# Three elementwise products of a layer moved from GpSimd to VectorE, and the recurrences' output, square and last-chain steps moved back in the order of work

## The chip, the cores and the metric

The kernel runs on one core of a Trainium2 chip. TensorE (PE) multiplies matrices into banks of PSUM; VectorE (DVE), ScalarE (ACT) and GpSimd (POOL) do elementwise work; SyncE (SP) issues most DMAs. Each engine works through its own instructions in a fixed order. The metric is the device time of one execution in microseconds; lower is better.

## The reference

One layer of a hybrid decoder, on 1024 positions of width 1024, in float32:

```
u     = rms_norm(x);  proj = u @ w_in             # 1024 -> 3584: q, k, v and hq, hf, hi, hg
attn  = rms_norm(dilated_attention(q, k, v))      # 8 heads of 64, three dilated windows merged
# HGRN2, 4 heads of 128, chunkwise:
forget = lb + (1 - lb) * sigmoid(hf);  b = cumsum(log(forget)) in a chunk
q_dec  = silu(hq) * exp(b);  k_inv = (1 - forget) * exp(-b)
rec    = tril(q_dec k_inv^T) @ hi + q_dec @ state;  state = decay * state + k_end^T @ hi
rec    = rms_norm(rec) * silu(hg)
h   = x + concat(attn, rec) @ w_out
h   = h + conv_glu(rms_norm(h))                   # 1024 -> 2 x 2816 -> 1024, causal conv of width 3
out = rms_norm(h)
```

## The kernel before, in words

Every float32 operand of a large product is split into an upper part (a rounded copy) and a lower part (what the copy leaves), and each product is three matmuls (upper by upper, upper by lower, lower by upper). ACT mostly makes the copies and DVE or POOL the subtractions. Activations lie transposed: 128 features on the partitions, 512 positions (a half, hf = 0 or 1) along a row.

The stages are: input projection and attention (0 to 303 us of the trace), the recurrences with their projections (303 to 484), the output projection (from 484, the last recurrences within it), the gated mixer up and down, and the final norm. PE's instructions run in the order in which the program writes them. The order on the other engines is planned ahead from a model of costs, among the instructions that the model holds ready, with those written earlier first; an instruction wrapped in `keep_in_program_order` stays behind the one written before it on its engine.

In the recurrence stage the filler work is 24 half projections (list HG: forget "hf", query "hq", gate "hg", 4 heads by 2 halves). Each is a `dense` of 24 matmuls into one of two banks ("mm"), which a DVE multiplication empties (L718, L732, L745). Behind it stand a sigmoid of three ACT activations (`sigmoid`, L708 to L710) and a product that makes the gate. Between the fillers the program puts the steps of eight recurrences, called chains 0 to 7 here, for (head, half) = (0,0), (0,1), (1,0), (1,1), (2,0), (3,0), (2,1), (3,1). A place is counted in half projections; `play` runs the filler up to a step's place and then writes the step. From place 24 on the filler is the output projection (`out_pair`). The five steps of a chain (`recur`) are:

1. scans over the log gates, differences, three exponentials on ACT (ex, C, A; L808, L811, L812), the query's product with the decay (E times C, L813) and the key's (B times A, L814);
2. four transposes (psK) and eight small matmuls of scores (psA); ACT copies kT, DVE masks into AT;
3. four matmuls for psU; DVE scales them and runs the state along the chunks (U, st; L839 to L847);
4. four or eight matmuls for the outputs psO, from AT and from st; ACT squares them (hsq, L860);
5. a matmul by ones sums the squares (hss, L863); ACT and DVE make the reciprocal root (`rstd_part`, L314 to L318), DVE scales psO by it (rhy, L865), POOL multiplies by the gate (L867).

The tiles rs_y (first st, then rhy) and rs_m (first U, then the square and rht) have one buffer each, so a chain's states wait for the tail of the chain before. The norm of the attention output (`attn_norm`) runs beside the first chains, at places 0.25 to 4.25 and 7 to 11; it makes the output projection's upper and lower operands attn_hi and attn_lo (L769 to L771). A chain of number n has at = 4.5 + 3n; its first step stood at the place just behind its query projection, step 2 at `at`, step 3 at `at + 1`, step 4 at `at + 2` (`at + 2.3` for chains 6 and 7) and step 5 at `at + 2.8`. For chain 0, steps 2 to 4 stood 0.5 later.

Of the kernel before, what the change touches and what calls it, by code (L numbers as in the profile page):

```python
# [12 lines left out]
AF = mybir.ActivationFunctionType  # L13
# [29 lines left out]
def f32(ap):  # L43
    return ap.bitcast(F32)
# [157 lines left out]
def hybrid_kernel(ctx: ExitStack, tc: tile.TileContext, xT, w_qk, w_tok, w_hg, w_out, w_up,  # L202
                  w_down, vecs, amask, hmask, out):
    nc = tc.nc
    PE, DVE, ACT, POOL = nc.tensor, nc.vector, nc.scalar, nc.gpsimd
# [93 lines left out]
    def col(j):  # L299
        return vec[:, j : j + 1]  # L300
# [24 lines left out]
    def vtile(shape, dt, name):  # L325
        return rv.tile(shape, dt, tag="v", name=name, bufs=2)
# [10 lines left out]
    def bank(tag, name):  # L337
        return ps1.tile([P, H2], F32, tag=tag, name=name, bufs=2)
# [4 lines left out]
    at = at_cm.__enter__()  # L343
# [347 lines left out]
    attn_lo = mix.tile([P, 4, SEQ], F32R, name="attn_lo")  # L691
    rec_hi0 = mix.tile([P, 4, H2], F32R, name="rec_hi0")
    def gtile(name, dt=F32):
        return mix.tile([P, H2], dt, tag="g", name=name, bufs=4)

    attn_hi = vtile([P, 4, SEQ], F32R, "attn_hi")
# [3 lines left out]
    with pool("hg", "right") as hg:  # L700
# [3 lines left out]
        def ht(tag, nm, bufs=1):  # L704
            return hg.tile([P, H2], F32, tag=tag, name=nm, bufs=bufs)

        def sigmoid(dst, src):
            ACT.activation(dst, src, AF.Exp, scale=-1.0)  # L708
            ACT.activation(dst, dst, AF.Ln, bias=1.0)
            ACT.activation(dst, dst, AF.Exp, scale=-1.0)  # L710
# [17 lines left out]
        def q_half(h, hf, last):  # L728
            def evac(ps):
                nm = f"{h}_{hf}"  # L730
                E, F = ht("E", "E" + nm, 2), ht("F", "F" + nm)
                DVE.tensor_mul(E, ps, R1[:, halves[hf]])  # L732
                DVE.tensor_scalar_max(F, E, -40.0)
                sigmoid(F, F)
                POOL.tensor_mul(E, E, F)
                gate[h, hf].append(E)
            return dense(("hq", h), hf, evac, last)

# [14 lines left out]
        def attn_norm(hf):  # L753
            t = halves[hf]
            acc, s2 = gtile(f"asq{hf}"), gtile(f"asq{hf}_s")
            ACT.activation(acc, raw[0, hf], AF.Square)
            for c in range(1, 4):
                ACT.activation(s2, raw[c, hf], AF.Square)
                DVE.tensor_add(acc, acc, s2)
            yield  # L760
            ss = bank("t", f"ass{hf}")
            PE.matmul(ss, ones, acc, start=True, stop=True)
            R = rstd_part(acc, s2, ss, 1.0 / 512)
            yield
            for c in range(4):
                if c == 2:
                    yield
                a = raw[c, hf]
                DVE.scalar_tensor_tensor(a, a, col(V_AG + c), R, op0=ALU.mult, op1=ALU.mult)  # L769
                ACT.copy(attn_hi[:, c, t], a)  # L770
                POOL.tensor_sub(attn_lo[:, c, t], a, f32(attn_hi[:, c, t]))  # L771
            yield


# [19 lines left out]
        def recur(h, hf):  # L794
            A, B, E = gate.pop((h, hf))
            nm = f"{h}_{hf}"

            C = ht("C", "C" + nm)
            C3 = C.rearrange("p (c t) -> p c t", c=4)
            for c in range(4):  # L800
                s = slice(c * P, (c + 1) * P)
                DVE.tensor_tensor_scan(C[:, s], ones, A[:, s], 0.0, op0=ALU.mult, op1=ALU.add)
            sm = hg.tile([P, 12], F32, tag="sm", name=f"sm{nm}", bufs=2)
            DVE.tensor_copy(sm[:, 0:4], C3[:, :, 63])
            DVE.tensor_copy(sm[:, 4:8], C3[:, :, 127])
            DVE.tensor_sub(sm[:, 8:12], sm[:, 4:8], sm[:, 0:4])
            ex = hg.tile([P, 12], F32, tag="ex", name=f"ex{nm}", bufs=2)
            ACT.activation(ex, sm, AF.Exp)  # L808
            A3 = A.rearrange("p (c t) -> p c t", c=4)
            DVE.tensor_sub(A3, C3, sm[:, 0:4].unsqueeze(2).to_broadcast([P, 4, P]))  # L810
            ACT.activation(C, A, AF.Exp)  # L811
            ACT.activation(A, A, AF.Exp, scale=-1.0)  # L812
            POOL.tensor_mul(E, E, C)  # L813
            DVE.tensor_mul(B, B, A)  # L814
            yield
            psA = bank("s", f"psA{nm}")
            psK = bank("t", f"psK{nm}")
            for c in range(4):
                s = slice(c * P, (c + 1) * P)
                PE.transpose(psK[:, s], B[:, s], ident)  # L820


            for c in range(4):
                s, s1 = slice(c * P, (c + 1) * P), slice(c * P, c * P + 64)
                PE.matmul(psA[0:64, s], B[:, s1], E[:, s], start=True, stop=True)
            for c in range(4):
                s, s2 = slice(c * P, (c + 1) * P), slice(c * P + 64, (c + 1) * P)
                PE.matmul(psA[64:128, s], B[:, s2], E[:, s2].unsqueeze(1).to_broadcast([P, 2, 64]), start=True, stop=True)
            kT = ht("kT", f"kT{nm}")
            ACT.copy(kT, psK)  # L830
            pA3 = psA.rearrange("p (c t) -> p c t", c=4)
            DVE.copy_predicated(AT, hm.unsqueeze(1).to_broadcast([P, 4, P]), pA3)
            yield
            psU = bank("s", f"psU{nm}")
            for c in range(4):
                s = slice(c * P, (c + 1) * P)
                PE.matmul(psU[:, s], kT[:, s], iv[:, 4 * hf + c, h * P : (h + 1) * P], start=True, stop=True)
            U = ht("rs_m", f"U{nm}").rearrange("p (c t) -> p c t", c=4)
            DVE.tensor_mul(U, psU.rearrange("p (c v) -> p c v", c=4), ex[:, 8:12].unsqueeze(2).to_broadcast([P, 4, P]))  # L839
            st = ht("rs_y", f"st{nm}").rearrange("p (c t) -> p c t", c=4)  # L840

            if hf:
                DVE.scalar_tensor_tensor(U[:, 0], state[h], ex[:, 4:5], U[:, 0], op0=ALU.mult, op1=ALU.add)
                DVE.tensor_scalar_mul(st[:, 0], state[h], ex[:, 0:1])
            for c in range(1, 4):
                DVE.scalar_tensor_tensor(U[:, c], U[:, c - 1], ex[:, 4 + c : 5 + c], U[:, c], op0=ALU.mult, op1=ALU.add)
                DVE.tensor_scalar_mul(st[:, c], U[:, c - 1], ex[:, c : c + 1])  # L847
            if hf == 0:
                state[h] = hg.tile([P, P], F32, tag="carry", name=f"carry{h}", bufs=2)
                POOL.tensor_copy(state[h], U[:, 3])  # L850
            yield
            psO = bank("o", f"psO{nm}")
            for c in range(4):
                s = slice(c * P, (c + 1) * P)
                no_state = hf == 0 and c == 0
                PE.matmul(psO[:, s], iv[:, 4 * hf + c, h * P : (h + 1) * P], AT[:, c], start=True, stop=no_state)
                if not no_state:
                    PE.matmul(psO[:, s], st[:, c], E[:, s], start=False, stop=True)
            sq = ht("rs_m", f"hsq{nm}")
            ACT.activation(sq, psO, AF.Square)  # L860
            yield
            ss = bank("t", f"hss{nm}")
            PE.matmul(ss, ones, sq, start=True, stop=True)  # L863
            R = rstd_part(ht("rs_y", f"rhy{nm}"), ht("rs_m", f"rht{nm}"), ss, 1.0 / P)
            DVE.scalar_tensor_tensor(R, psO, col(V_HG + h), R, op0=ALU.mult, op1=ALU.mult)  # L865
            g_ = G[h, hf]
            POOL.tensor_mul(g_, R, g_)  # L867
            yield
            yield
# [21 lines left out]
        place = {x[:3]: i + 1 for i, x in enumerate(HG)}  # L891
        steps = []

        def rec_steps(h, hf):
            chain = iter(())

            def first():
                nonlocal chain
                chain = recur(h, hf)
                next(chain)  # L900

            yield first
            while True:
                yield lambda: next(chain, None)

        for n, (h, hf) in enumerate(((0, 0), (0, 1), (1, 0), (1, 1), (2, 0), (3, 0), (2, 1), (3, 1))):
            at = 4.5 + 3 * n
            late = 0.5 if n == 0 else 0.0
            end = 2.3 if n > 5 else 2.0
            steps += zip((place["hq", h, hf], at + late, at + 1 + late, at + end + late, at + 2.8), rec_steps(h, hf))  # L910
        for hf in range(2):
            norm = attn_norm(hf)
            steps += [(6.75 * hf + x, lambda norm=norm: next(norm, None)) for x in (0.25, 2.25, 3.25, 4.25)]
# [256 lines left out]
    with pool("ps2", "left", space=PSUM) as ps2:  # L1170
# [46 lines left out]
        for f in range(2, NFF):  # L1217
            end = up(f, sums)
# [232 lines left out]
```

## Time and profile before

| | |
|---|---|
| runs shown | 1246.98, 1248.61 and 3455.92 us, median 1248.61 |
| profiled execution | 1246.1 us, its span 1244.3 us |
| PE busy | 1214.4 us (98% of the span) |
| DVE busy | 958.2 us (77%) |
| ACT busy | 633.9 us (51%) |
| POOL busy | 341.7 us (27%) |
| DMA | 122.39 MB, 98 GB/s on average |

The page gives the busy time of each engine and cuts the span into slices. A view of waits says for whom an engine stood still; a timeline shows the instructions in order, each with its start, its length and, in brackets, the idle time before it and what ended that.

### The profile page before, as it was taken

The page shows a single profiled execution, that of the slowest core. Times are in us where ns is not written, and L with a number is a line of the kernel's source. Part 1 is how long each engine was busy: PE and PEld are TensorE (multiplying, and loading weights), DVE is VectorE, ACT ScalarE, POOL GpSimd, SP SyncE. Part 2 cuts the span into 40 slices and gives each one's busy share as a digit, 9 for nine tenths or more (in the row PEclk, how much of TensorE's full clock was granted, in tenths as well). Part 3 has the DMA queues.
Part 4 walks back from the last instruction along what each step waited for, and adds up shares of the span by engine and source line. Part 5 has one row for each costly group of instructions (what it writes and reads, how often), then busy time and mean ns, then how long its engine had stood idle before and what let it go on. Part 6 is the DMA issues. An engine that isn't in the chain of part 4 may idle for free. (4 is left out here: it accounts for less than half of the span.)

```text
span 1244.3 us, 17799 instructions
## 1 busy us (share of the span) xinstructions
PE 1214.4 (98%) x6192; PEld 1024.1 (82%) x6192; DVE 958.2 (77%) x1756; ACT 633.9 (51%) x1153; POOL 341.7 (27%) x310
## 2 busy tenths in 40 slices
PE   9999999999999998999999999999999999999996
PEld 7898889998777787888778888888888878888886
DVE  8867776556867776564899988888888878957986
ACT  8566666676555655443554343434434344444542
POOL 1164444563314224614212223222222210000000
PEclk9999999999989999999999999999999999999999
DMA  7021111233111212344022233332233257535522
GB/s 251 22 68 52 55 56 52 77 95 95 35 34 35 68 52 77 110 144 135 9 70 97 91 107 119 110 112 83 94 110 119 102 169 262 155 100 158 172 89 89
DMA packets 67721, 122.39 MB, mean 98 GB/s; under 512 B 7344, under 2 KB 9648, under 8 KB 67632
## 3 DMA queue, kind: packets, MB, share of 16 engines
q1 hardware_dynamic: 56832, 101.80, 26.0%
q10 hardware_dynamic: 10800, 19.47, 4.1%
q8 instruction: 48, 0.79, 0.3%
q14 instruction: 41, 0.34, 0.1%
HBM read 97.65 MB, written 23.59 MB: 97 GB/s over the span
## 5 line engine op out<-in xcount | busy, mean ns | idle before, releaser
L87 POOL TENSOR_TENSOR wlo<-raww,whi 128x512 fp32r<-128x512 f32 x141 | 207.8, 1486 | 376.0 <-ACT whi L85 271.4
L85 ACT CAST whi<-raww 128x512 fp32r<-128x512 f32 x276 | 168.9, 618 | 203.0 <-DVE raww L119 53.2
L87 DVE TENSOR_TENSOR wlo<-raww,whi 128x512 fp32r<-128x512 f32 x136 | 101.4, 746 | 19.6 <-ACT whi L85 19.3
L85 ACT CAST whi<-r 128x512 fp32r<-128x512 f32 x70 | 43.6, 623 | 85.1 <-PE ds L1345 42.0
L542 POOL TENSOR_SCALAR P<-P,st 128x512 f32<-128x512 f32 (+2 forms) x96 | 55.4, 587 | 113.5 <-DVE st L539 73.1
L533 DVE CUSTOM_DVE_ANT_0 P<-S,mask 128x512 f32<-128x512 f32 (+2 forms) x96 | 52.0, 552 | 25.1 <-PE S L531 24.2
L569 DVE TENSOR_TENSOR tl<-T,th 128x512 fp32r<-128x512 f32 (+1 forms) x80 | 50.8, 635 | 21.9 <-ACT th L568 20.8
L538 ACT ACTIVATE P<-P,st 128x128 f32<-128x128 f32 (+3 forms) x64 | 49.6, 776 | 33.4 <-DVE st L537 18.8
L1321 POOL TENSOR_TENSOR facc<-facc,sqf 128x256 f32<-128x256 f32 x4 | 2.9, 731 | 226.7 <-ACT sqf L1320 226.6
L87 DVE TENSOR_TENSOR wlo<-r,whi 128x512 fp32r<-128x512 f32 x70 | 48.0, 687 | 21.8 <-ACT whi L85 21.7
L1058 PE MATMUL p<-b1h,whi 128*128 128x512 f32 x160 | 62.4, 390 | 0.6 <-DVE a L1089 0.6
L1344 PE MATMUL ds<-fhi,whi 128*128 128x512 f32 x160 | 62.6, 392 | 0.0
L1080 DVE SCALAR_TENSOR_TENSOR cv<-g,vec,cv 128x511 f32<-128x511 f32 (+1 forms) x92 | 56.5, 615 | 7.9 <-ACT cv L1077 6.9
L1059 PE MATMUL p<-b1l,whi 128*128 128x512 f32 x160 | 62.3, 389 | 0.0
L1346 PE MATMUL ds<-fhi,wlo 128*128 128x512 f32 x160 | 62.2, 389 | 0.0
L1345 PE MATMUL ds<-flo,whi 128*128 128x512 f32 x160 | 62.2, 389 | 0.0
L1060 PE MATMUL p<-b1h,wlo 128*128 128x512 f32 x160 | 62.2, 389 | 0.0
L568 ACT CAST th<-T 128x512 fp32r<-128x512 f32 (+1 forms) x80 | 43.0, 537 | 23.5 <-PE T L561 20.3
L85 ACT CAST fhi<-rawf 128x512 fp32r<-128x512 f32 x70 | 43.2, 617 | 15.4 <-DMA rawf<-spT 5.2
L87 DVE TENSOR_TENSOR flo<-rawf,fhi 128x512 fp32r<-128x512 f32 x70 | 48.0, 686 | 2.8 <-ACT fhi L85 2.8
L1345 PE MATMUL da<-flo,whi 128*128 128x512 f32 x120 | 46.9, 391 | 1.6 <-DVE flo L87 1.6
L1087 ACT ACTIVATE cv<-cv 128x512 f32<-128x512 f32 x44 | 27.9, 633 | 38.7 <-DVE cv L1080 38.7
(660 smaller groups left out, 3959.8 us busy)
## 6 DMA issues: line engine op xcount, KB each, us to landing
raww<-in_w_up_dram SPq DMA_DIRECT2D x88, 256.0 KB, 3.0
raww<-in_w_tok_dram SPq DMA_DIRECT2D x52, 256.0 KB, 2.8
rawf<-spT SPq DMA_DIRECT2D x40, 256.0 KB, 2.7
r<-in_w_down_dram SPq DMA_DIRECT2D x40, 256.0 KB, 3.7
raww<-in_w_hg_dram SPq DMA_DIRECT2D x32, 256.0 KB, 2.6
raww<-in_w_out_dram SPq DMA_DIRECT2D x32, 256.0 KB, 2.6
spB<-a ACTq DMA_DIRECT2D x30, 256.0 KB, 2.4
spT<-t ACTq DMA_DIRECT2D x30, 256.0 KB, 2.0
```

The lines of the kernel that those rows point to most:

```text
L85: self.pin(self.high(hi[:, :w], raw))
L87: self.pin(low.tensor_sub(lo[:, :w], raw, f32(hi[:, :w])))
L533: DVE.tensor_tensor_reduce(Pt[:, k0 : k0 + w], S[:, :w], mask[:, m : m + w], -1.0, BIG * 3, op0=ALU.add, op1=ALU.min, accum_out=st[:, k0 / ...
L542: POOL.tensor_scalar(e, e, st[:, 3:4], 1.0, op0=ALU.mult, op1=ALU.mult)
L569: DVE.tensor_sub(tl[:, :n], T[:, :n], f32(th[:, :n]))
L1058: PE.matmul(ps, hi[:, s], bhi, start=(start and n == 0), stop=False)
L1059: PE.matmul(ps, hi[:, s], blo, start=False, stop=False)
L1060: PE.matmul(ps, lo[:, s], bhi, start=False, stop=(stop and n == len(rhs) - 1))
L1080: DVE.scalar_tensor_tensor(dst, x, col(V_CW + j * NFF + f), dst, op0=ALU.mult, op1=ALU.add)
L1344: PE.matmul(ps[d], hi[:, s], ahi, start=(k == 0), stop=False)
L1345: PE.matmul(ps[d], hi[:, s], alo, start=False, stop=False)
L1346: PE.matmul(ps[d], lo[:, s], ahi, start=False, stop=(k == NPAIR - 1))
```

## The change

- The query's two products (silu, L735, and the product with the decay, L813) and the lower part of the attention output (L771) run on DVE, not on POOL. The gate's product (L748), the tail's product (L867) and the copy of the carried state stay on POOL.
- Step 4 of every chain stands at `at + 2.2` and step 5 at `at + 3.1`, which is behind step 2 of the next chain (`at + 3`); for chain 0 the shift of 0.5 holds for step 5 too.
- Chain 7 runs 0.5 places later, and its first step stands at 24.9 (`at - 1.1`), not at 24. Its three exponentials are kept behind the ACT instruction written before them.

```diff
@@ q_half @@
-                POOL.tensor_mul(E, E, F)
+                DVE.tensor_mul(E, E, F)
@@ attn_norm @@
-                POOL.tensor_sub(attn_lo[:, c, t], a, f32(attn_hi[:, c, t]))
+                DVE.tensor_sub(attn_lo[:, c, t], a, f32(attn_hi[:, c, t]))
@@ recur @@
-            ACT.activation(ex, sm, AF.Exp)
+            order = tc.keep_in_program_order if (h, hf) == (3, 1) else lambda ins: ins
+            order(ACT.activation(ex, sm, AF.Exp))
...
-            ACT.activation(C, A, AF.Exp)
-            ACT.activation(A, A, AF.Exp, scale=-1.0)
-            POOL.tensor_mul(E, E, C)
+            order(ACT.activation(C, A, AF.Exp))
+            order(ACT.activation(A, A, AF.Exp, scale=-1.0))
+            DVE.tensor_mul(E, E, C)
@@ the order of the steps @@
-            at = 4.5 + 3 * n
-            late = 0.5 if n == 0 else 0.0
-            end = 2.3 if n > 5 else 2.0
-            steps += zip((place["hq", h, hf], at + late, at + 1 + late, at + end + late, at + 2.8), rec_steps(h, hf))
+
+            at = 4.5 + 3 * n + 0.5 * (n in (0, 7))
+            start = at - 1.1 if n == 7 else place["hq", h, hf]
+            steps += zip((start, at, at + 1, at + 2.2, at + 3.1), rec_steps(h, hf))
```

## Rows read from the trace of the kernel before

**Rows 1.** The page's busy times: us, share of the span, instructions.

```profile
PE 1214.4 (98%) x6192; PEld 1024.1 (82%) x6192; DVE 958.2 (77%) x1756; ACT 633.9 (51%) x1153; POOL 341.7 (27%) x310
```

**Rows 2.** Busy time by stretch; behind the engines come PE's clock, DMA share, GB/s.

```profile
300.00:540.00 240.00, 229.75 (x1159) 187.90 (x1158) 168.98 (x302) 130.58 (x236) 85.86 (x67) 0.99 0.21 66
340.00:350.00 10.00, 8.61 (x35) 7.34 (x36) 8.01 (x16) 6.39 (x11) 2.09 (x3) 0.83 0.16 52
350.00:360.00 10.00, 7.45 (x32) 5.31 (x31) 5.99 (x14) 5.55 (x9) 0.96 (x2) 0.83 0.00 0
...
490.00:500.00 10.00, 7.00 (x37) 5.22 (x36) 5.78 (x14) 6.72 (x13) 5.92 (x5) 1.00 0.43 132
```

**Rows 3.** PE's waits, whole span: us in total, times, longest.

```profile
PE hss L863 <- ACT hsq L860: 5.5, 2, 3.0
PE p__hf___1_0_4321 L428 <- DVE G L745: 2.6, 1, 2.6
PE psO L858 <- DVE st L847: 2.1, 4, 1.4
```

**Rows 4.** PE's timeline: start, us, line, xcount; first matmuls of two half projections.

```profile
325.54 0.39 PE L428 MATMUL p__hg___0_0_4204<-uhi,whi 128*128 128x512 f32 x1
...
330.98 0.39 PE L428 MATMUL p__hg___0_1_4259<-uhi,whi 128*128 128x512 f32 x1
```

**Rows 5.** ACT's timeline, 491 to 498 us.

```profile
495.84 0.63 ACT L812 ACTIVATE A<-A 128x512 f32<-128x512 f32 x1
496.37 0.58 ACT L860 ACTIVATE hsq<-psO 128x512 f32<-128x512 f32 x1
```

**Rows 6.** Groups by line and shape, 302 to 540 us: count, busy us, mean ns.

```profile
L813 POOL TENSOR_TENSOR E<-E,C 128x512 f32<-128x512 f32 x8 | 11.7, 1466 | 3.0 <-ACT C L811 2.5
...
L810 DVE TENSOR_TENSOR A<-C,sm 128x512 f32<-128x512 f32 x8 | 5.5, 689 | 0.0
```

**Rows 7.** Timelines of DVE and PE: last recurrence part and its first reader.

```profile
527.39 0.69 DVE L878 TENSOR_TENSOR rl<-G,rec_hi 128x512 fp32r<-128x512 f32 x1 [2.49 <-ACT rec_hi L877]
...
547.01 0.39 PE L962 MATMUL po<-rec_hi,whi 128*128 128x512 f32 x1
```

**Rows 8.** POOL's timeline, 325 to 341 us.

```profile
330.43 4.53 POOL L771 TENSOR_TENSOR attn_lo<-raw,attn_hi 128x512 fp32r<-128x512 f32 x3
```

**Rows 9.** DVE's timeline beside it, and the same scans at 357 us.

```profile
323.90 1.42 DVE L769 SCALAR_TENSOR_TENSOR raw<-raw,vec,asq 128x512 f32<-128x512 f32 x2
...
325.83 3.49 DVE L769 SCALAR_TENSOR_TENSOR raw<-raw,vec,asq 128x512 f32<-128x512 f32 x2
329.24 0.68 DVE L732 TENSOR_TENSOR E<-p__hq___0_1_4137,R 128x512 f32<-128x512 f32 x1
...
330.94 1.51 DVE L733 TENSOR_SCALAR F<-E 128x512 f32<-128x512 f32 x1
332.38 4.55 DVE L802 TENSOR_TENSOR_SCAN C<-ones,A 128x128 f32<-128x128 f32 x4
...
341.35 0.43 DVE L746 TENSOR_SCALAR Fg<-G 128x512 f32<-128x512 f32 x1
...
357.74 1.37 DVE L802 TENSOR_TENSOR_SCAN C<-ones,A 128x128 f32<-128x128 f32 x4 [0.88 <-ACT A L724]
```

**Rows 10.** Timelines of PE and POOL: chains 1 to 3.

```profile
380.56 1.02 PE L863 MATMUL hss<-hsq,ones 128*128 128x512 f32 x2
...
404.13 1.08 PE L863 MATMUL hss<-hsq,ones 128*128 128x512 f32 x2
...
414.05 1.05 PE L837 MATMUL psU<-iv,kT 128*128 128x128 f32 x8
...
420.39 0.38 PE L856 MATMUL psO<-AT,iv 128*128 128x128 f32 x2
...
395.40 1.30 POOL L867 TENSOR_TENSOR G<-rhy,G 128x512 f32<-128x512 f32 x1 [1.63 <-DVE rhy L865]
...
413.61 1.58 POOL L867 TENSOR_TENSOR G<-rhy,G 128x512 f32<-128x512 f32 x1 [8.70 <-DVE rhy L865]
```

## The prediction

> **What bounds the kernel now.** I read the page's busy times first, then the busy time by stretch, then who waited for whom on the matrix engine PE, and last the timelines of the stretches where PE stood still. PE is busy for 98% of the span [rows 1], so a change can win only what PE loses by waiting or by its clock. The changed code lies between 300 and 540 us. There PE is busy for 229.75 of 240 us, so 10.25 us are idle, and VectorE (DVE) is idle for 71 us [rows 2]. In two of the ten-microsecond slices shown the granted clock is 0.83, not 1.00: part of those slices ran at 1.2 GHz where 2.4 GHz is full speed [rows 2]. Each lost 10 x (1 - 0.83) = 1.7 us on top of its idle time. All that this stage can give is 10.25 + 2 x 1.7 = 13.65 us.
>
> Three of PE's waits matter [rows 3]. Call them A, B and D, with C for the last line. A: the forget projection of head 1 waits 2.6 us for a bank that DVE empties late (L745). B and D: the sum over the squares (hss, L863) waits for ScalarE's (ACT's) square of the output (L860), 5.5 us in two waits, the longer of 3.0 us being D, so B is 2.5 us. C: the outputs (psO) wait for the states that DVE makes (L847), 2.1 us in four waits. The two slices of low clock hold A and B. D lies in the slice at 490 us, whose clock stayed at 1.00 [rows 2], so a wait of this size costs its idle time surely and the 1.7 us only sometimes.
>
> One place in the order of work is one half projection, 24 matmuls: 330.98 - 325.54 = 5.44 us [rows 4].
>
> **The steps of the recurrences.** Chain 0's outputs stood at place 7.0 and its hss at 7.3, so 0.3 x 5.44 = 1.6 us of matmuls lay between, and B followed. They now stand at 7.2 and 8.1. Chain 1's transposes and scores, at 7.5, fall between as well, so the cover is 4.9 us plus that block, against 1.6 + 2.5 us that were needed. I take B as gone, with its clock loss: 2.5 + 1.7 = 4.2 us.
>
> D belongs to chain 6. Its gap grows from 0.5 to 0.9 places, 2.2 us more cover, which leaves 0.8 of 3.0 us. The rest comes from ACT's queue: the square at 496.37 stood directly behind the last chain's exponential at 495.84 [rows 5]. The last chain now begins at place 24.9, behind chain 6's outputs at 24.7, and its three exponentials are held behind the ACT instruction written before them. So D goes whole, 3.0 us (bounds 2.2 and 3.0). The last chain then has 1.1 places, 6.0 us, from its beginning to its transposes; its two products of 0.69 us [rows 6] and two exponentials of 0.63 us [rows 5] need 2.6 us. Its end moves by 0.8 places, 4.4 us: the last low part was made at 527.39 and that half of the recurrences is first multiplied at 547.01 [rows 7]. I cost that at nothing. No moved step issues a DMA, so SP's queue keeps its order; on POOL's queue the moved steps have one product each (L867), behind fewer others than before.
>
> **The products moved to VectorE.** There are 24: eight each of the query product (L735), the product with the decay (L813) and the lower part (L771). One took 1.47 us on POOL; DVE's comparable subtraction takes 0.69 us [rows 6]. That adds 24 x 0.69 = 16.6 us to DVE, which has 71 us idle. What matters is where it lands, and whether POOL's share had been slowing DVE. While POOL ran products without a gap [rows 8], a pair of DVE operations took 3.49 us against 1.42 for the same pair just before, a pass over one tile 1.51 against 0.43, and four scans 4.55 against 1.37 in a quiet stretch [rows 9]. That is 2.07 + 1.08 + 3.18 = 6.3 us lost. In the same stretch DVE's read of a matmul bank (L732) took its usual 0.68 us [rows 9].
>
> Ahead of A's release DVE gets seven of the products (four L771, two L735, one L813), 4.8 us, and gets back 6.3. A shrinks by 1.5 us of its 2.6, and I count half of its clock loss: 1.5 + 0.85 = 2.4 us. The bounds are all of it, 2.6 + 1.7 = 4.3 us, and, with nothing given back, 4.8 us worse. I take the value near the upper bound because the lost time is measured in that very stretch. The new waits of DVE for ACT (third exponential, exp of the decay, copy of the upper part) queue the emptying of banks behind them; PE notices only when a bank is later than a whole half projection, which is A's case and is counted there. The lower parts are made by about place 11 and read only by the output projection, at place 24: 13 places, 70 us, of half projections stay their cover.
>
> The Trainium skill (SBUF — State Buffer, Who interferes with whom) says that a VectorE operation with two SBUF inputs, or in a two-port mode, and a GpSimd operation that reads SBUF exclude each other, one blocking for the other's whole length, while an operation with one SBUF input outside those modes is untouched. The trace agrees in kind: the bank read kept its 0.68 us and the others stretched. By the rule DVE would get back nearly all of POOL's time in that stretch, A would vanish, and the sum below would be 1.9 us lower.
>
> **What the later steps cost.** A chain's tail runs from hss over ACT and DVE to POOL's product (L867); that frees the buffer in which the next chain's states are written, which its psO waits for. The tail began 9.9 us before the next chain's psU (404.13 to 414.05) and 16.3 us before its psO (420.39) [rows 10]. Now hss stands behind the next chain's transposes, and psO 0.2 later: 2.1 places, 11.4 us, plus hss 1.0 and psU 0.8 make 13.2 us. The slack falls by 3.1 us. Of the tails of chains 0 to 5, the fast one shown took 413.61 + 1.58 - 404.13 = 11.1 us, the slowest 395.40 + 1.30 - 380.56 = 16.1 us [rows 10]. Add 0.6 us for the first two states, and allow 0.45 us because PE has intra-chunk products first. Then 11.1 fits within 13.65, and 16.1 overshoots by 3.0 us. For chain 0 to chain 1 the room is 1.6 places + 1.0 + 0.8 + 1.0 = 11.5 us, plus 0.3, tight even for the fast tail. I expect one slow tail: waits at psO of 3.0 us in place of C's 2.1, so 0.9 us worse. Bounds: 2.1 better (none), and 5 x 3.0 + 4.9 - 2.1 = 17.8 worse (all slow).
>
> **Sum.** -4.2 (B) - 3.0 (D) - 2.4 (A) + 0.9 (C) = -8.7 us. The profiled execution took 1246.1 us, which gives 1237.4. The median of the runs is 2.5 us above that execution; I allow 1.6 and forecast 1239 us.
>
> **Rivals.**
> 1. DVE becomes the late engine. Nothing is given back, since POOL keeps the gate products, L867 and some lower parts of weights, and A grows by 4.8 us: -4.2 - 3.0 + 4.8 + 0.9 = -1.5, so about 1246 with the same allowance. For it: DVE was already the releaser in A and C. Against: the 6.3 us lost. Chance 0.2.
> 2. Slower: the tails. If they all run at 16.1 us, the state buffer is free too late in every chain: +17.8 - 4.2 - 3.0 - 2.4 = +8.2, so about 1256 us. It decides once the mean tail passes 14.7 us (5 waits of x - 13.05 and one of x - 11.2 then eat up the 9.6 us won and C's 2.1). For it: hss now comes just behind the next chain's scores, whose copy and exponentials want ACT too, and DVE has 24 more instructions ahead of the tail's three. Against: the fast tail was measured with POOL's collisions in it, and its product waits behind fewer others on POOL. Chance 0.13.
> 3. The change doesn't do what it says: ACT's order comes out such that the squares again stand behind exponentials that wait. B and D stay in part, say 4 us of idle and one clock loss: -8.7 + 5.7 = -3, about 1245 us. Against: B's and D's cover grows whatever ACT does. Chance 0.07.
>
> **Numbers.** The forecast's own case has 0.6 and reaches from 1234 (all 13.65 us won, with the allowance) to 1243. Rivals 1 and 3 end below 1248, and the tails at half of rival 2's price give 1247. The range 1233 to 1249 leaves out most of rival 2 and the edges of the others, under 2 in 10. Two per cent is 25 us, about what a measurement of this kernel can tell from no change: more than the stage can give back, and three times rival 2's loss. So faster 0.01, within 0.97, slower 0.02.
>
> **What would show it.** Right: no wait of hss for the square; the slices around B and D full, and at clock 1.00; A below 1.5 us; the scans' mean near 343 ns; DVE busy in the stage at most a few us higher. C would show as psO waits of 0 to 4 us. Wrong: psO waits of 3 us in several chains with tails above 14.7 us (rival 2), or bank waits on L718, L732 or L745 that grow (rival 1). A new fall of the clock would add 1.7 us to any of them.

## The result and the profile after

The changed kernel takes 1239.47 us (median of six runs, 1238.88 to 1239.96), the kernel before 1247.09 us beside it: 7.6 us less by the medians and 6.5 us by the ratio of 0.9948 (interval 0.9938 to 0.9958). One of the six runs of the kernel before (3455.92 us), and further below one run of products_only (1507.21 us at a granted clock of 0.751), were slow and count in no ratio. The forecast was 1239 us. The number came out, but not by its own sum: the changed steps won 6 us more than the sum had, and a wait that it didn't hold took 8 us back. This section shows both; the experiments then separate them.

From L808 on the changed kernel's lines have numbers higher by one (hss L863 is L864). Its busy times by engine:

```profile
PE 1210.2 (98%) x6192; PEld 1022.5 (83%) x6192; DVE 950.4 (77%) x1780; ACT 637.8 (52%) x1153; POOL 309.7 (25%) x286
```

Its busy times by stretch (columns as in [rows 2]), the recurrence stage first, then the start of the mixer:

```profile
300.00:540.00 240.00, 240.00 (x1223) 197.85 (x1222) 174.66 (x342) 141.84 (x249) 56.48 (x44) 1.00 0.24 75
340.00:350.00 10.00, 10.00 (x54) 8.45 (x53) 7.76 (x14) 5.45 (x10) 2.54 (x3) 1.00 0.08 26
350.00:360.00 10.00, 10.00 (x57) 8.06 (x56) 6.33 (x15) 6.70 (x13) 0.00 (x0) 1.00 0.15 43
490.00:500.00 10.00, 10.00 (x50) 8.40 (x49) 3.89 (x11) 3.12 (x5) 5.67 (x6) 1.00 0.23 67
600.00:620.00 20.00, 15.28 (x68) 12.33 (x66) 20.00 (x34) 9.59 (x16) 3.38 (x1) 1.00 0.19 66
620.00:640.00 20.00, 14.93 (x55) 12.19 (x56) 13.40 (x23) 6.02 (x11) 4.26 (x3) 0.75 0.16 54
```

In the stage PE never stands still, where it stood for 10.25 us before [rows 2], and the two slices of low clock are at 1.00. DVE's busy time in this window rose by 5.7 us (168.98 to 174.66), but the window holds more of the program's work than before, because the changed kernel is ahead. From the stage's start to the time at which DVE empties one and the same tile in the mixer (the first p1v, below), the kernel before and then the changed one show:

```profile
300.00:631.19 331.19, 320.54 (x1550) 260.99 (x1548) 234.15 (x400) 177.75 (x312) 107.03 (x79) 0.99 0.23 71
```

```profile
299.60:615.12 315.52, 315.13 (x1550) 258.74 (x1548) 228.76 (x424) 180.16 (x312) 75.94 (x55) 1.00 0.24 75
```

PE's 1550 matmuls are the same, 24 instructions have gone from POOL to DVE, and DVE's busy time for it all fell, by 5.4 us. Behind the stage, though, two stretches of 20 us miss 4.7 and 5.1 us, the second at a granted clock of 0.75. PE's longest waits in the whole span show why; none of those of [rows 3] is left, and one is new:

```profile
PE p L1059 <- DVE a L1090: 9.8, 1, 9.8
PE T L557 <- DVE tl L569: 1.5, 1, 1.5
```

PE's timeline around it, the last matmul of one product and the first of the next:

```profile
614.89 0.39 PE L1061 MATMUL p1v<-b22h,wlo 128*128 128x512 f32 x1
625.07 0.80 PE L1059 MATMUL p<-b1h,whi 128*128 128x512 f32 x1 [9.79 <-DVE a L1090]
625.66 0.63 PE L1060 MATMUL p<-b1l,whi 128*128 128x512 f32 x1
...
630.27 0.40 PE L1059 MATMUL p<-b22h,whi 128*128 128x512 f32 x1
```

The same place in the kernel before:

```profile
630.93 0.39 PE L1060 MATMUL p1v<-b22h,wlo 128*128 128x512 f32 x1
631.92 0.50 PE L1058 MATMUL p<-b1h,whi 128*128 128x512 f32 x1 [0.60 <-DVE a L1089]
```

Up to 614.89, against 630.93, the changed kernel had won 16.0 us. There PE then stood 9.8 us and worked on at half clock (a granted clock of 0.50 from 620 to 630 us, which is 1.2 GHz): 12 matmuls take 625.07 to 630.27, 5.2 us, where the usual 0.23 us apart would make 2.8. That is 9.8 + 2.4 = 12.2 us lost, against 0.6 us at this place before. (0.7 and 0.43 us of small waits behind it, which the kernel before has, are gone.)

What PE waits for is a bank. The mixer's third feature opens a new pool of PSUM banks, and its first product p takes the pool's first bank. Before, that bank had held the first of two value products (p1v of half 0); now it holds the second. Bank numbers stand in no view of the profile: this was read from the built program, and the turned kernels below test it. The trace shows the two times at which DVE empties a p1v. In the changed kernel:

```profile
615.12 0.68 DVE L1090 TENSOR_TENSOR a<-p1v,cv 128x512 f32<-128x512 f32 x1
...
624.33 0.68 DVE L1090 TENSOR_TENSOR a<-p1v,cv 128x512 f32<-128x512 f32 x1
```

and in the kernel before:

```profile
631.19 0.67 DVE L1089 TENSOR_TENSOR a<-p1v,cv 128x512 f32<-128x512 f32 x1
...
640.43 0.68 DVE L1089 TENSOR_TENSOR a<-p1v,cv 128x512 f32<-128x512 f32 x1
```

DVE's order here is the same in both and merely stands 16.1 us earlier (631.19 to 615.12), and it has no gap (20.00 of 20 us busy). So DVE was not made late. Before, p followed the emptying at 631.19; now it follows the one at 624.33, 9.2 us behind the one at 615.12. The pair of banks called "t" serves, among others, the transposes psK, the sums hss and these two value products in turn, and by the built program the turn comes out the other way with the steps moved.

### The profile page after: what moved, and what is told of

It is laid out like the page before. It is cut to its first block, busy times and chain, and to the rows that moved or that the text cites. A ratio compares the mean times of both kernels' runs of the same rounds, so it can differ in the third digit from the quotient of the medians.

```text
span 1237.8 us, 17779 instructions
## 1 busy us (share of the span) xinstructions
PE 1210.2 (98%) x6192; PEld 1022.5 (83%) x6192; DVE 950.4 (77%) x1780; ACT 637.8 (52%) x1153; POOL 309.7 (25%) x286
## 5 line engine op out<-in xcount | busy, mean ns | idle before, releaser
L87 POOL TENSOR_TENSOR wlo<-raww,whi 128x512 fp32r<-128x512 f32 x141 | 206.3, 1474 | 394.0 <-ACT whi L85 300.6
L87 DVE TENSOR_TENSOR wlo<-raww,whi 128x512 fp32r<-128x512 f32 x136 | 100.0, 736 | 23.3 <-ACT whi L85 23.0
L87 DVE TENSOR_TENSOR wlo<-r,whi 128x512 fp32r<-128x512 f32 x70 | 47.9, 686 | 22.0 <-ACT whi L85 21.9
L87 DVE TENSOR_TENSOR flo<-rawf,fhi 128x512 fp32r<-128x512 f32 x70 | 47.9, 685 | 3.4 <-ACT fhi L85 3.4
L1347 PE MATMUL da<-fhi,wlo 128*128 128x512 f32 x120 | 46.8, 390 | 0.1
```

Of the source, the lines that this page charges most:

```text
L87: self.pin(low.tensor_sub(lo[:, :w], raw, f32(hi[:, :w])))
L1347: PE.matmul(ps[d], lo[:, s], ahi, start=False, stop=(k == NPAIR - 1))
```

## The experiments

Two edits make both kernels use equal banks. "Turned" takes one more tile from the pair "t" ahead of the value products, for a matmul of four columns:

```diff
     p1 = {("g", 0): p1, ("g", 1): bank("o", "p1g1")}
+    PE.matmul(bank("t", "turn")[:, :4], ones, ones[:, :4], start=True, stop=True)
```

"Free bank" puts the second value product into another pair:

```diff
-        p1["v", hf] = bank("t", f"p1v{hf}")
+        p1["v", hf] = bank("mm" if hf else "t", f"p1v{hf}")
```

**after_turned**, the changed kernel turned:

> The changed kernel with one tiny extra matmul (4 columns) into the pair of banks 't' ahead of feature 1's value products, so that the pair's rotation is turned by one and the first value product, not the second, lies in the bank that feature 2's first product takes. Theory 'bank': the 9.8 us wait there becomes about 0.6, its low clock (2.4 us) goes, two small waits for weights (1.1 us) come back: 1239.5 - 9.2 - 2.4 + 1.1 = about 1229 us. Theory 'VectorE-bound': PE only reached a stretch early in which VectorE is 100% busy, and some other wait of VectorE's takes the place: about 1239 us.

Measured 1230.75 us (1229.88 to 1231.59), ratio to before 0.9876, interval 0.9862 to 0.989. The first matmul of p now waits for the earlier emptying:

```profile
615.69 0.50 PE L1059 MATMUL p<-b1h,whi 128*128 128x512 f32 x1 [0.37 <-DVE a L1090]
```

DVE is as full as before, so a full VectorE was not the reason. The bank was. This kernel has the lowest median of all here, 15 us below before and 8.7 us below the change as it stands.

**before_turned**, the kernel before turned:

> The kernel before with the same tiny matmul, which turns its rotation the other way, into the unlucky place. Theory 'bank': its wait of 0.6 us at feature 2's first product becomes about 9.8 us, with the low clock behind it, and the two small waits for weights go: 1247 + 9.2 + 2.4 - 1.1 = about 1257.5 us. Theory 'VectorE-bound': no change, about 1247 us.

Measured 1256.66 us, ratio 1.0087, interval 1.0073 to 1.01. The wait appears in a kernel that has nothing of the change; its longest waits:

```profile
PE p L1058 <- DVE a L1089: 9.6, 1, 9.6
PE hss L863 <- ACT hsq L860: 6.1, 2, 3.1
```

**after_free_bank** and **before_free_bank**:

> The changed kernel with feature 1's second value product in the pair 'mm', whose bank feature 2 takes last (for feature 3's first product): no bank of feature 2's first products is emptied late. Theory 'bank': about 1228 us, and the stage of the recurrences as in the changed kernel, without a wait. Theory 'VectorE-bound': about 1239 us.

> The kernel before with the same bank for feature 1's second value product: the base of the further comparisons. Theory 'bank': its first value product still lies in the bank that feature 2 takes first, as before, so 1247 us within 1 us. Theory 'VectorE-bound': also 1247 us.

Measured 1231.52 us (ratio 0.9881, interval 0.9867 to 0.9895) and 1246.51 us (0.9999, 0.9988 to 1.0009). In the first, PE is busy in the stage without a gap:

```profile
300.00:540.00 240.00, 240.00 (x1224) 197.85 (x1223) 174.73 (x342) 141.85 (x249) 56.40 (x44) 1.00 0.24 75
```

So on equal banks the change is worth 15.0 us, not the 8.7 of the sum, and the bank takes back 8 of them. That is less than the 12.2 us lost at it, and 1231.52 us is more than the 1228 expected. With the free bank PE meets another wait at once: 1.6 us for an upper part (whi) from ACT, at 619.71, and the slice from 620 to 630 us has a granted clock of 0.83. The kernels that follow all have the free bank, so that this wait does not cover their differences.

**places_only**: the steps moved, all 24 products left on POOL.

```diff
-                DVE.tensor_mul(E, E, F)
+                POOL.tensor_mul(E, E, F)
...
-                DVE.tensor_sub(attn_lo[:, c, t], a, f32(attn_hi[:, c, t]))
+                POOL.tensor_sub(attn_lo[:, c, t], a, f32(attn_hi[:, c, t]))
...
-            DVE.tensor_mul(E, E, C)
+            POOL.tensor_mul(E, E, C)
```

> Base: the two kernels with the free bank (before 1246.5, changed 1231.5 us). This one has the changed places, order and held exponentials, but all 24 products back on POOL. By the prediction's terms: the two waits for the square gone (-7.2 us), the bank wait A of 2.6 us still there, tails longer (psO waits of 3 us, +0.9): about 1240 us. Theory 'places': they carry the whole gain, and with them A goes too: about 1232 us. Theory 'products': POOL's products were behind all the waits, so nothing is won here: about 1246 us.

Measured 1240.24 us, ratio 0.9951, interval 0.9937 to 0.9964: 6.1 us faster than before. The stage and its waits:

```profile
300.00:540.00 240.00, 233.38 (x1187) 190.60 (x1186) 166.09 (x306) 136.69 (x241) 87.38 (x67) 1.00 0.22 70
```

```profile
PE p__hf___1_0_4321 L428 <- DVE G L745: 2.6, 1, 2.6
...
PE psU L838 <- ACT kT L831: 1.4, 1, 1.4
...
PE p__hf___2_0_4742 L428 <- DVE G L745: 1.1, 1, 1.1
...
PE psO L859 <- DVE st L848: 1.0, 3, 0.6
PE psO L859 <- DVE st L845: 0.5, 1, 0.5
```

No wait of hss is left: the places alone end B and D. A stays, as large as before. New small waits have come, but at psU and a bank of head 2, and those of psO are smaller than before. DVE's timeline ahead of A's release is that of the kernel before [rows 9] to 0.2 us:

```profile
329.44 0.68 DVE L732 TENSOR_TENSOR E<-p__hq___0_1_4137,R 128x512 f32<-128x512 f32 x1
330.05 1.18 DVE L87 TENSOR_TENSOR wlo<-raww,whi 128x512 fp32r<-128x512 f32 x1
331.14 1.51 DVE L733 TENSOR_SCALAR F<-E 128x512 f32<-128x512 f32 x1
332.57 4.55 DVE L802 TENSOR_TENSOR_SCAN C<-ones,A 128x128 f32<-128x128 f32 x4
...
339.60 1.25 DVE L815 TENSOR_TENSOR B<-B,A 128x512 f32<-128x512 f32 x1 [1.47 <-ACT A L813]
340.77 0.68 DVE L745 TENSOR_TENSOR G<-p__hg___0_0_4204,R 128x512 f32<-128x512 f32 x1
```

In the changed kernel the same work and eight products more end 5 us earlier:

```profile
329.05 0.42 DVE L802 TENSOR_TENSOR_SCAN C<-ones,A 128x128 f32<-128x128 f32 x1
329.38 0.40 DVE L733 TENSOR_SCALAR F<-E 128x512 f32<-128x512 f32 x1
329.70 1.05 DVE L802 TENSOR_TENSOR_SCAN C<-ones,A 128x128 f32<-128x128 f32 x3
...
335.80 0.68 DVE L745 TENSOR_TENSOR G<-p__hg___0_0_4204,R 128x512 f32<-128x512 f32 x1
```

**products_only** and **products_again**: the kernel before with its 24 products on DVE and every step at its old place. They are one kernel under two labels; its waits are read from the second.

> Same base. The places and order of before, with all 24 products on VectorE. By the prediction's terms: A shrinks to about 1 us (-2.4 us), the waits for the square of 2.5 and 3.0 us stay: about 1244 us. Theory 'products': all waits shrink, about 1232 us. Theory 'places': 1246.5 us, or more where VectorE is now later (rival 1: A grows to 7 us, about 1251).

> The kernel before with its 24 products on VectorE and feature 1's second value product in the other bank; steps at their old places. It was 1235.9 us, 4.4 us above the whole change (1231.5), and this look is for its waits. If the moved products release the squares sooner as well, D's wait (3.0 us) is gone and at most B stays: B's 2.5 us with its 1.7 us of clock is 4.2 us, the whole distance. If the products only take away A, as the prediction had it, both waits of hss stay at about 5.5 us together and PE's busy time in 300 to 540 us is near 234 of 240 us, too little for 1235.9.

Measured 1235.89 us (ratio 0.9908, interval 0.9894 to 0.9922) and 1235.3 us (0.9914, 0.9894 to 0.9934): 11 us faster than before. Its wait in the stage is that of hss alone; below it the stage, and the slices that had A and B:

```profile
PE hss L863 <- ACT hsq L860: 3.2, 2, 2.0
```

```profile
300.00:540.00 240.00, 236.79 (x1198) 194.06 (x1197) 169.65 (x335) 137.32 (x244) 53.73 (x43) 0.99 0.23 71
340.00:350.00 10.00, 8.17 (x43) 6.66 (x42) 7.56 (x14) 5.47 (x10) 2.34 (x3) 1.00 0.09 26
350.00:360.00 10.00, 9.85 (x45) 7.32 (x46) 7.03 (x16) 6.23 (x12) 0.00 (x0) 0.83 0.07 28
```

Neither account held whole: B shrank to 2.0 us and kept its low clock, and D was not gone but fell from 3.0 to 1.2 us. A and C are gone. The products alone do more than the prediction gave to all parts together.

**low_parts_on_pool**: the whole change, but the eight lower parts on POOL (the second of the three edits above).

> Same base. The whole change but for the eight lower parts of the attention output, which stay on POOL. They are what ran beside VectorE's scans ahead of A. If POOL's products slow VectorE by their length, the scans at that point stretch again (four in about 4 us, not 1.4) and A comes back with 1 to 3 us and perhaps its clock loss of 1.7: 1233 to 1236 us. If the query's products were what mattered, no wait: 1231.5 us.

Measured 1235.09 us, ratio 0.9908, interval 0.9894 to 0.9922: 3.6 us behind the whole change. A has not come back, and the scans are not stretched (four in 0.41 and 1.04 us), but a bank of the projection before is late, and psO waits:

```profile
PE psO L859 <- DVE st L848: 1.3, 2, 0.7
PE p__hg___0_1_4259 L428 <- DVE E L732: 1.1, 1, 1.1
```

What makes L732 late is a collision in its plainest form, three DVE operations beside three POOL products (DVE's timeline, then POOL's):

```profile
326.38 1.78 DVE L769 SCALAR_TENSOR_TENSOR raw<-raw,vec,asq 128x512 f32<-128x512 f32 x1
328.09 1.78 DVE L814 TENSOR_TENSOR E<-E,C 128x512 f32<-128x512 f32 x1
329.80 1.77 DVE L87 TENSOR_TENSOR wlo<-raww,whi 128x512 fp32r<-128x512 f32 x1
331.49 0.68 DVE L732 TENSOR_TENSOR E<-p__hq___0_1_4137,R 128x512 f32<-128x512 f32 x1
```

```profile
326.19 4.83 POOL L771 TENSOR_TENSOR attn_lo<-raw,attn_hi 128x512 fp32r<-128x512 f32 x3 [22.80 <-ACT attn_hi L770]
```

They go one for one: 1.71 us from one DVE operation to the next, where the same operations in the changed kernel follow each other every 0.60 to 0.65 us.

**query_on_pool**: the whole change, but the query's 16 products on POOL (the first and third edits).

> The whole change with the second value product in the other bank (1231.5 us), but the query's two products (16) on GpSimd; the 8 lower parts stay on VectorE. All 24 on GpSimd were 1240.2, the lower parts alone there 1235.1. If the products' shares add up, the query's two are worth 8.7 - 3.6 = 5.1 us: 1236.6. If the lower parts are what stretched the scans ahead of A and the rest is free, 1231.5 to 1233. If any product on GpSimd in that stretch is enough for A to come back, 2.6 us and its clock: about 1236.

Measured 1233.91 us, ratio 0.9906, interval 0.9891 to 0.9921: 2.4 us behind the whole change by the medians, less than the 5.1 of equal shares. The losses are small waits of psO, these and one of 0.5 us for L845, and A isn't among them:

```profile
PE psO L859 <- DVE st L848: 1.8, 3, 0.9
```

The two kernels lose 3.6 and 2.4 us, together 6.0; with all 24 on POOL it is 8.7. Either group may stay without A coming back; both together bring it back.

**outputs_early**, **squares_early** and **last_chain_early**: the whole change with one of the moves of places undone.

```diff
-            steps += zip((start, at, at + 1, at + 2.2, at + 3.1), rec_steps(h, hf))
+            steps += zip((start, at, at + 1, at + 2.0, at + 3.1), rec_steps(h, hf))   # outputs_early
+            steps += zip((start, at, at + 1, at + 2.2, at + 2.8), rec_steps(h, hf))   # squares_early
```

```diff
-            order = tc.keep_in_program_order if (h, hf) == (3, 1) else lambda ins: ins
+            order = lambda ins: ins                       # last_chain_early
...
-            at = 4.5 + 3 * n + 0.5 * (n in (0, 7))
-            start = at - 1.1 if n == 7 else place["hq", h, hf]
+            at = 4.5 + 3 * n + 0.5 * (n == 0)
+            start = place["hq", h, hf]
```

> Same base. The whole change but with the outputs at 'at + 2.0' as before (the squares' sum still at 3.1). It tests the room for the states: 0.2 places, 1.1 us less between psU and psO. By the prediction's account of the tails (a fast tail fits, slow ones overshoot by 3 us) the waits of psO come back, 1 to 4 us in all: 1232.5 to 1236 us. If the tails are short of the room by more than that, no wait: 1231.5 us.

> The whole change with the second value product in the other bank (1231.5 us), but hss again at `at + 2.8` (chain 0 at 3.3), 0.6 places behind the outputs and ahead of the next chain's transposes. By the prediction's account the squares came 3.6 to 4 us behind the outputs, against a cover of 3.3 us: small waits of hss in several chains, 1 to 4 us in all, 1233 to 1235. If the products on VectorE have made the squares sooner, no wait comes back: 1231.5.

> The whole change with the second value product in the other bank (1231.5 us), but chain 7 begins at its old place 24 with its transposes at 25.5, and its exponentials are not held. The prediction gave 0.8 of D's 3.0 us to this part and 2.2 us to the later hss: by it D comes back with 0 to 1 us, 1231.5 to 1232.5. If the square again stands behind the last chain's exponentials, hss or psO waits 2 to 3 us: 1233.5 to 1236.

Measured 1232.33 us (ratio 0.9883, interval 0.9868 to 0.9899), 1231.52 us (0.9882, 0.9868 to 0.9897) and 1231.67 us (0.9881, 0.9864 to 0.9897): none can be told from the whole change. Each leaves one short wait in the stage: psO 0.8 us in the first, hss 0.4 in the second, psK 0.8 in the third. Undone all together, as in products_again, they cost some 4 us. So with the products on DVE no single one of the three is needed: the other two hold the square and the states off the path.

## Why the prediction came out, and where it was wrong

**B and D, the places: right.** Their terms, -4.2 and -3.0 with C's +0.9, make -6.3; places_only measured -6.1. That no wait of hss would remain, the full slices around B and D and the clock of 1.00 all held. That the sums agree so closely is in part luck: PE's idle time in the stage fell by only 3.6 us (10.25 to 6.62), because C came out worse than priced, while in the profiled execution A's clock loss of 1.7 us did not occur although A's wait stayed, which no term had. How D goes was split too finely: the prediction gave 2.2 us to the later hss and the rest to the last chain's later start, while with the products on DVE each of the two does without the other (the 0.4 us in squares_early stand at chain 3, at 416.70, not at chain 6).

**C: twice the price, and at other waits.** With the places alone, psU and a bank of head 2 waited for 2.5 us and psO for 1.5, where psO had waited for 2.1 [rows 3]: 1.9 us worse, not 0.9, and mostly not at the wait that was named. In the whole change nothing of it is left, since the tails are short. From hss to the end of POOL's product they take 7.9 to 11.9 us, 9.8 in the mean of chains 0 to 5, where rival 2 needed a mean of 14.7. One of them, chain 2's, on PE and POOL:

```profile
396.51 1.12 PE L864 MATMUL hss<-hsq,ones 128*128 128x512 f32 x2
```

```profile
404.31 2.54 POOL L868 TENSOR_TENSOR G<-rhy,G 128x512 f32<-128x512 f32 x1 [10.37 <-DVE rhy L866]
```

**The products, the step that failed.** The prediction gave them -2.4 us ("A shrinks by 1.5 us of its 2.6"); alone they are worth 11, and 8.7 on top of the places. It failed twice.

First, in the account ahead of A's release. It set 4.8 us of new work against 6.3 us given back. The rows of places_only against those of the changed kernel give 7.6 us back: the four scans 3.3, the pair of L769 2.1, L733 1.1, and also L87 and L815 with 0.5 and 0.6, which the prediction had not looked at. Another 1.5 us is DVE's wait for ACT's second exponential, which ends as well. The products ahead of the release are eight, not seven: the second product with the decay (L813 on POOL at 338.83 in the kernel before) was left out of the count. They cost 8 x 0.60 = 4.8 us, not 8 x 0.69, because one starts every 0.60 us though a record is 0.69 long. 7.6 + 1.5 - 4.8 = 4.3 us earlier. L745 starts at 335.80 instead of 340.77, 5.0 us, of which 0.6 had been won before this stretch (the pair of L769 ahead of it starts at 323.50, not 324.10): 4.4 us are left. A is gone, with its clock loss.

Second, I priced the products only where A is. The same collisions stood in every chain, so C's states and the tails and squares came sooner too: products_again has C's 2.1 us gone and 5.5 us of hss down to 3.2. The sign named for the scans, a mean near 343 ns, was mis-stated. 343 ns is a quarter of the 1.37 us that four scans take one behind the other, and the mean of the records fell from 503 to 406 ns. The spread shows that no scan is held up any more (shortest, median and longest record in ns, before and after):

```profile
L802 DVE TENSOR_TENSOR_SCAN C<-ones,A x32: 392/399/1491, 313.5 to 492.0; 128x128 f32<-128x128 f32 x32
```

```profile
L802 DVE TENSOR_TENSOR_SCAN C<-ones,A x32: 393/400/425, 313.1 to 478.9; 128x128 f32<-128x128 f32 x32
```

The Trainium skill (SBUF — State Buffer, Who interferes with whom) says that a VectorE operation with two SBUF inputs and a GpSimd operation that reads SBUF exclude each other, and by it, the prediction says, A would vanish. The trace agrees: in low_parts_on_pool one DVE operation passed per POOL product, and in the kernel before the read of a bank (L732, at 329.24 [rows 9]) kept its 0.68 us in the middle of one:

```profile
328.73 1.74 POOL L813 TENSOR_TENSOR E<-E,C 128x512 f32<-128x512 f32 x1
```

The rule should have been the forecast for A. The rest of what the products won lies in the other chains, which the prediction did not price.

**The bound of the stage was too low.** "All that this stage can give" was 13.65 us, yet 16.0 were won by the mixer's start, 0.4 of them ahead of the stage. A record of a matmul lasts 0.16 us longer than the distance to the next, so each listed wait is short by about that: seven waits of [rows 3] make 1.1 us. The remaining 0.9 us I can't place.

**The bank, not foreseen.** Of the 15 us, 8 were lost some 100 us behind the last step that was moved (chain 7's product on POOL ends at 515.15, the wait begins at 615.28). No case of the prediction had it: rival 1 looked for a late DVE in the stage, and DVE was in time there and no later in the mixer. On equal banks the change is a gain of 15 us, outside the forecast's own case and outside its range, so 1239 us was met because a sum 6.3 us too small and an allowance of 1.6 us happened to make up for the bank's 8. Which one of the moved steps turns the pair was not tried.

**Rivals.** 1 fell: DVE's busy time for the same work fell by 5.4 us, and no bank wait on L718, L732 or L745 is left. 2 fell by the tails. 3 fell: in the whole change no hss waits at all.

## What to carry to other kernels

Price a product on POOL by what it takes from a busy DVE: here 1.71 - 0.60 = 1.1 us, more than the 0.60 us that DVE needs to do it itself, and count that in every chain, not only at the worst wait. Not every product meets a DVE operation: by the estimate in the next section DVE got back 0.8 us for each of the 24. When steps that take tiles from a rotating set of banks are reordered, look up who inherits which bank in the next stage, and compare the first waits behind the changed code: a single dummy tile was worth 8.7 us. Where several moves aim at the same wait, undo each alone before crediting any of them.

## What the runs showed of the hardware

Handing DVE 24 operations of 0.60 us, 14.4 us of work, lowered its busy time for the same piece of the program by 5.4 us (234.15 to 228.76). A record's length holds the time in which the operation is held up beside the other engine: about 1.78 us for each of the three beside POOL's products, against 0.69 to 0.75 for the same lines in the changed kernel. As an estimate from these numbers, 14.4 + 5.4 = 19.8 us were given back, 0.8 us for each product moved.

The clock doesn't follow a wait's length. Behind 2.0 us at hss in products_again PE ran at half speed (0.83 in that slice); in places_only the 2.6 us of A cost no clock, its slice being at 1.00:

```profile
340.00:350.00 10.00, 8.41 (x44) 7.24 (x45) 8.00 (x16) 6.44 (x12) 2.09 (x3) 1.00 0.17 52
```

Before, the same wait of 2.6 us in the same place was followed by a slice at 0.83 [rows 2]. Further on in that run of places_only PE waited only 1.6 us for an upper part (at 629.26), and the slice from 630 to 640 us was at 0.83. A term for the clock can thus only be given as one that may or may not come with a wait. It also varies between runs of one kernel: beside after_turned the kernel before took 1244.14 us at a mean granted clock of 0.998 and 1249.47 us at 0.991.
